# Rotary turns six steps later, a table operation in another step, value evictions on two engines, and the inverse's predicated copies ahead of the low parts

## The chip, the cores and the metric

The kernel runs on one core of a Trainium2 chip. The metric is the time of one execution on the device, in microseconds (us); lower is better. The five engines are named as the profile names them: PE is TensorE (matmuls; PEld are its weight loads), DVE is VectorE, ACT is ScalarE, POOL is GpSimd, and SP is SyncE, which issues the DMAs. Each works through its own queue in order, and they wait for each other on semaphores.

## What is computed

The reference is a two-layer encoder on 256 tokens of width 2048. Each layer normalises, projects all channels by one large matrix, and sends the result to two groups of heads:

```python
for l in range(DEPTH):
    h = rms_norm(x, norm_g[l])
    proj = jnp.einsum('btd,dc->btc', h, w_in[l])
    rw_in, g_rw, q, k_at, v_at, g_at = jnp.split(proj, col_splits, axis=-1)
    ...
    y_rw = rwkv7_branch(r, k, v, xw, xa, ...)
    qh = rope(q.reshape(B, T, AT_HEADS, HEAD_DIM), positions)
    kh = rope(k_at.reshape(B, T, AT_KV_HEADS, HEAD_DIM), positions)
    y_at = window_attention(qh, kh, vh, sink[l]).astype(x.dtype)
    mix = jnp.concatenate([y_rw * jax.nn.silu(g_rw), y_at * jax.nn.silu(g_at)], axis=-1)
    x = x + jnp.einsum('btc,cd->btd', mix, w_out[l])
return rms_norm(x, final_g)
```

The first group is a recurrence over time (16 heads, both directions), the second a windowed attention with rotary positions on q and k: with `t1`, `t2` the halves of a head, the result is `t1 cos - t2 sin` and `t2 cos + t1 sin`.

## The kernel before

**Weights as two parts.** All large products run in a format that keeps fewer bits than float32, so both operands are split in a high and a low part, and each step of a product is three matmuls: high weights by high and by low activations, low weights by high activations (`pm` at L291, L292, L293). A weight tile of 128 rows and 1024 columns arrives by DMA (`raw`, three buffers, L213); `wsplit` then makes its halves: ACT copies 512 columns to `hi` (L221), DVE subtracts to get `lo` (L223). `hi` and `lo` have two buffers each, and one tile feeds eight steps.

**The stream and its windows.** The weight products form one long stream of steps, `S`. The rest (recurrence, attention) is cut into generators. A window runs 64 steps in 14 groups; lists of group numbers say when a generator's next piece is emitted, and TensorE runs in exactly this order (`manual_schedule`). On the other engines a scheduler chooses the order, by the place in the program and by priorities: `tc.high_priority(offset=n)` moves what stands in it ahead, `PRIO_LO = 40` for the low parts and `PRIO_B = 95` for the last stage of the recurrence. What goes through `PA` and `PV` (ACT and DVE by way of `keep_in_program_order`, L236 in the profile) keeps the program's order among itself. `S.later(n, fn)` emits `fn` when n more steps have run.

**The recurrence's inverse.** Ten windows, one for each pair of heads and two for the start, feed three stages: `scan_p` prepares operands, `scan_i` inverts triangular 64x64 blocks, `scan_b` runs the chain over four chunks. The inversion doubles the block size in six levels. Of each level TensorE computes `pq` (L897; transposes at L864), ACT copies it to `QF` (L900) and `tt` (L868), TensorE computes `pd` (L906), and DVE puts `pd` into the block `TC` (tile `tv`) under a mask: `copy_predicated`, L907. The next level's L897 reads `tv`; after the last level L864 does, for `pf`. `scan_b` has `rh` (L956), `suv` (L972 on ACT, L979 on DVE), the product L977, and at its end a variance `yv` (L996, then a power on POOL, L997) and the normalised `ysq`.

**Rotary positions.** When the product of a k or q tile is done, `rope_evac` copies it from PSUM to `raw` (a tile named `u`, L532), issues four DMAs that exchange the halves of the heads into `rrot` (L534, one buffer), and leaves two functions for later: `turn` after 7 steps (two multiplies and an add on DVE) and `parts` after 10 (high part on ACT, low part on DVE). There are ten such tiles in each layer; the next tile's product ends 16 steps after, or 32 where a gate's tile lies between.

**Values.** `v_step` accumulates two tiles `pva` in the two PSUM buffers that all products of the stream share; `v_evac` scales both into `VA` on DVE (L569). The stream's next product takes the first one's buffer.

**Tables.** Sine and cosine are made once, in layer 0, by a generator `setup` of many small DVE operations (tiles `VA`, `SIN`, `COS`); `ROT` and its default list tell in which groups of a window its next operation is emitted.

## Time and profile before

| | us |
|---|---|
| median of three runs | 1202.62 (1201.23 to 1203.34) |
| the profiled execution | 1201.32 |
| its span, first to last instruction | 1199.5 |
| PE busy | 1165.4 |
| DVE busy | 910.2 |
| ACT busy | 776.3 |
| POOL busy | 18.9 |

The granted TensorE clock is 0.991 of full speed on average. A row of the timeline has the start in us, the duration, engine and line, the operation with its output, `<-` and its inputs, the count, and in brackets how long the engine idled before it and what released it. An idle time before a matmul is counted from the modelled end of the one before. `x2` behind a row means two instructions merged, with their joint time.

### The profile page before, as it was taken

How to read it: one execution, taken by the hardware profiler on the slowest of the kernel's cores; microseconds unless marked ns; L12 is line 12 of the kernel's file. 1: busy time of each engine (PE TensorE's matmuls, PEld its weight loads, DVE VectorE, ACT ScalarE, POOL GpSimd, SP SyncE). 2: the span in 40 equal slices, each digit the busy share in tenths (PEclk: the TensorE clock that was granted, in tenths of full speed). 3: DMA queues.
4: the chain of work that ended last, by engine and by line, in shares of the span. 5: the costliest groups of instructions: out<-in, count | busy, mean ns of one | idle time of the engine just before them, and what ended most of it. 6: DMA issues, size and time to landing. Idle time of an engine off the chain costs nothing. (4 is left out here: it accounts for less than half of the span.)

```text
span 1199.5 us, 38085 instructions
## 1 busy us (share of the span) xinstructions
PE 1165.4 (97%) x16151; PEld 1087.2 (91%) x16151; DVE 910.2 (76%) x2019; ACT 776.3 (65%) x1953; POOL 18.9 (2%) x23
## 2 busy tenths in 40 slices
PE   8999999999999999999999999999999999999996
PEld 6998999999888889999999989999998888889996
DVE  6888888888876668866667978887887766786554
ACT  6666776777776557655555766876777665665553
POOL 0000000000000000000000000000000000000000
PEclk8999999999999999999999999999999999999998
DMA  7553333323333434467655443334323333345653
GB/s 254 163 174 124 107 100 114 118 85 115 110 105 106 129 98 137 143 221 249 214 183 166 133 129 113 100 106 127 115 92 99 116 115 131 113 148 186 212 186 121
DMA packets 60410, 166.63 MB, mean 139 GB/s; under 512 B 7728, under 2 KB 22736, under 8 KB 60240
## 3 DMA queue, kind: packets, MB, share of 16 engines
q1 hardware_dynamic: 60240, 164.21, 42.5%
q8 instruction: 126, 2.06, 0.7%
q14 instruction: 44, 0.36, 0.1%
HBM read 157.37 MB, written 4.19 MB: 135 GB/s over the span
## 5 line engine op out<-in xcount | busy, mean ns | idle before, releaser
L291 PE MATMUL pm<-XH,hi 128*128 128x256 f32 x1664 | 495.9, 298 | 3.4 <-ACT XH L183 1.7
L293 PE MATMUL pm<-XH,lo 128*128 128x256 f32 x1664 | 469.9, 282 | 6.2 <-DVE lo L223 6.2
L292 PE MATMUL pm<-XL,hi 128*128 128x256 f32 x1664 | 469.4, 282 | 0.3
L221 ACT ACTIVATE hi<-raw 128x512 fp32r<-128x512 f32 x560 | 327.7, 624 | 194.9 <-PE pm L292 110.3
L223 DVE TENSOR_TENSOR lo<-raw,hi 128x512 fp32r<-128x512 f32 x560 | 369.7, 686 | 97.5 <-ACT hi L221 91.3
L291 PEld LDWEIGHTS pm<-XH,hi 128*128 128x128 f32 x1664 | 315.0, 189 | 18.5 <-ACT XH L183 2.4
L293 PEld LDWEIGHTS pm<-XH,lo 128*128 128x128 f32 x1664 | 315.4, 190 | 8.8 <-DVE lo L223 8.5
L292 PEld LDWEIGHTS pm<-XL,hi 128*128 128x128 f32 x1664 | 315.4, 190 | 1.1 <-DVE XL L184 1.1
L291 PE MATMUL pm<-MH,hi 128*128 128x256 f32 x512 | 144.1, 281 | 0.0
L293 PE MATMUL pm<-MH,lo 128*128 128x256 f32 x512 | 144.0, 281 | 0.0
L292 PE MATMUL pm<-ML,hi 128*128 128x256 f32 x512 | 143.8, 281 | 0.0
L291 PEld LDWEIGHTS pm<-MH,hi 128*128 128x128 f32 x512 | 96.6, 189 | 0.8 <-issue 0.8
L293 PEld LDWEIGHTS pm<-MH,lo 128*128 128x128 f32 x512 | 96.6, 189 | 0.2 <-DVE lo L223 0.2
L292 PEld LDWEIGHTS pm<-ML,hi 128*128 128x128 f32 x512 | 96.6, 189 | 0.0
L907 DVE CAST_PREDICATED tv<-LV,pd 128x256 f16<-128x256 uint8 x80 | 34.4, 430 | 12.8 <-PE pd L906 12.2
L790 DVE TENSOR_TENSOR ge<-pg,C 128x1024 f32<-128x1024 f32 x32 | 38.9, 1221 | 4.4 <-PE pg L784 4.4
L972 ACT ACTIVATE suv<-pcc 64x128 f32<-64x128 f32 x128 | 34.2, 267 | 11.4 <-PE pcc L970 7.1
L900 ACT ACTIVATE QF<-pq 128x256 f16<-128x256 f32 x80 | 30.8, 384 | 14.3 <-PE pq L864 13.8
L1062 ACT ACTIVATE mv<-mv,mx 128x257 f32<-128x257 f32 x64 | 31.8, 501 | 11.3 <-DVE mx L1059 11.3
L956 ACT ACTIVATE rh<-pcc 128x128 f32<-128x128 f32 x64 | 17.5, 273 | 33.2 <-PE pcc L954 32.8
L784 PE MATMUL pg<-mv,bk 64*128 64x128 f32 x512 | 37.2, 285 | 0.3 <-DVE ge L790 0.3
L784 PEld LDWEIGHTS pg<-mv,bk 64*128 64x128 f32 x512 | 31.1, 187 | 2.4 <-DVE ge L790 0.4
(247 smaller groups left out, 1860.1 us busy)
## 6 DMA issues: line engine op xcount, KB each, us to landing
raw<-wi SPq DMA_DIRECT2D x207, 512.0 KB, 3.8
raw<-wo SPq DMA_DIRECT2D x64, 512.0 KB, 4.2
raw<-wv SPq DMA_DIRECT2D x8, 512.0 KB, 3.7
rrot<-u SPq DMA_DIRECT2D x80, 32.0 KB, 2.1
vg<-xT SPq DMA_DIRECT2D x16, 128.0 KB, 4.2
xd<-vg SPq DMA_DIRECT2D x16, 128.0 KB, 3.5
vg<-xd SPq DMA_DIRECT2D x16, 128.0 KB, 3.7
g<-dup SPq DMA_DIRECT2D x16, 97.0 KB
```

The source lines that it names most:

```text
L221: A.activation(hi[:, q], raw[:, q], AF.Copy)
L223: V.tensor_tensor(lo[:, q], raw[:, q], hi[:, q].bitcast(F32), op=ALU.subtract)
L291: PE.matmul(pm, wh, rh[:, kk, :], start=(kk == 0), stop=False)
L292: PE.matmul(pm, wh, rl[:, kk, :], start=False, stop=False)
L293: PE.matmul(pm, wl, rh[:, kk, :], start=False, stop=(kk == 15))
L784: PE.matmul(pg[:, h, c * 128 : (c + 1) * 128], BK[half[h], d, c, 1 - h : 3 - h, :].rearrange("p s j -> p (s j)"), MV[half[h], d, c].rearra ...
L790: V.tensor_tensor(GEd(d), pg.rearrange("p h (c x) -> p h c x", c=NC), gm[d].unsqueeze(1).unsqueeze(1).to_broadcast([128, 2, NC, 128]), op= ...
L900: A.activation(t_sub(QF), flat4(pq[:, :, 0:128]), AF.Copy)
L907: V.copy_predicated(t_sub(TC), t_mask, flat4(pd[:, :, 0:128]))
L956: A.activation(RH, pc[:, 0], AF.Copy)
L972: A.activation(here(h), pc[half[h], 1], AF.Copy)
L1062: A.activation(Sc[:, h, q, 0:257], Sc[:, h, q, 0:257], AF.Exp, scale=0.125, bias=mx[:, q : q + 1], accum_out=den[:, q : q + 1])
```

## The change

```diff
+PRIO_TC = 400
...
-                S.later(7, turn)
-                S.later(10, parts)
+                S.later(13, turn)
+                S.later(15, parts)
...
             L.VA = st("VA", [2, 256])
-            for b in range(2):
-                V.tensor_scalar(L.VA[:, b, :], pvs[b], L.norm.rt[:, b : b + 1], None, op0=ALU.mult)
+            with tc.high_priority(offset=PRIO_B):
+                A.activation(L.VA[:, 0, :], pvs[0], AF.Copy, scale=L.norm.rt[:, 0:1])
+                V.tensor_scalar(L.VA[:, 1, :], pvs[1], L.norm.rt[:, 1:2], None, op0=ALU.mult)
...
-                V.copy_predicated(t_sub(TC), t_mask, flat4(pd[:, :, 0:128]))
+                with tc.high_priority(offset=PRIO_TC):
+                    V.copy_predicated(t_sub(TC), t_mask, flat4(pd[:, :, 0:128]))
...
-            window(64, *scans(w), *([(setup_, ROT.get(w, [3, 6, 9, 12]))] if l == 0 else []))
+            window(64, *scans(w), *([(setup_, ROT.get(w, [3, 6, 12, 12]))] if l == 0 else []))
```

`turn` and `parts` come 6 and 5 steps later. Of the two value tiles ACT evicts the first and DVE the second, both at a raised priority. The five predicated copies of levels two to six have a priority above the low parts and above `scan_b`. In the windows that use the default list (the third to the seventh, counted from one), the table operation of group 9 goes to group 12, where another follows it. The lines of the changed kernel are up to three higher than before, so L907 is L910 there, L223 is L224 and L236 is L237. TensorE's and POOL's instructions keep their order; on SyncE two or three weight loads change places with other DMAs. DVE and ACT change order in the windows concerned.

On DVE at the end of the ninth window of layer 0 (354 to 364 us in the trace) the rows before are these; `u` and `rrot` are the first k tile's rotation, `kd` its low part:

```order
L236 SCALAR_TENSOR_TENSOR lw<-lw,PR,kr 128x256
L996 TENSOR_SCALAR yv<-yv 128x4
L236 TENSOR_TENSOR u<-u,TW 128x256
L236 TENSOR_TENSOR rrot<-rrot,XA 128x256
L236 TENSOR_TENSOR u<-u,rrot 128x256
L223 TENSOR_TENSOR lo<-raw,hi 128x512
L236 TENSOR_TENSOR kd<-u,KA 128x256
L236 TENSOR_TENSOR ysq<-py,yv 128x256
L223 TENSOR_TENSOR lo<-raw,hi 128x512
L907 COPY_PREDICATED tv<-LV,pd 128x2x4x32
```

The same place on DVE in the changed kernel:

```order
L237 SCALAR_TENSOR_TENSOR lw<-lw,PR,kr 128x256
L999 TENSOR_SCALAR yv<-yv 128x4
L237 TENSOR_TENSOR ysq<-py,yv 128x256
L224 TENSOR_TENSOR lo<-raw,hi 128x512 x2
L910 COPY_PREDICATED tv<-LV,pd 128x2x4x32
L237 TENSOR_TENSOR th<-lw,th 128x256
L237 TENSOR_TENSOR u<-u,TW 128x256
L237 TENSOR_TENSOR rrot<-rrot,XA 128x256
L237 TENSOR_TENSOR u<-u,rrot 128x256
```

The rotation moved from ahead of `ysq` and the last copy to behind them.

On DVE in the middle of the third window (104 to 109 us), before; `kr` and `u` are an input tile's eviction and `lw` the bonus of the recurrence:

```order
L236 TENSOR_TENSOR mv<-kr,pp 128x8x64
L433 TENSOR_TENSOR u<-pm,rb 128x256
L907 COPY_PREDICATED tv<-LV,pd 128x2x8x16
L236 TENSOR_TENSOR lw<-lw 128x256
L435 SCALAR_TENSOR_TENSOR kr<-u,PR,kr 128x255
L236 SCALAR_TENSOR_TENSOR lw<-lw,PR,kr 128x256
L436 SCALAR_TENSOR_TENSOR kr<-u,PR,kr 128x255
L223 TENSOR_TENSOR lo<-raw,hi 128x512 x2
```

The same place on DVE in the changed kernel:

```order
L237 TENSOR_TENSOR mv<-kr,pp 128x8x64
L910 COPY_PREDICATED tv<-LV,pd 128x2x8x16
L434 TENSOR_TENSOR u<-pm,rb 128x256
L237 TENSOR_TENSOR lw<-lw 128x256
L224 TENSOR_TENSOR lo<-raw,hi 128x512
L436 SCALAR_TENSOR_TENSOR kr<-u,PR,kr 128x255
L237 SCALAR_TENSOR_TENSOR lw<-lw,PR,kr 128x256
L437 SCALAR_TENSOR_TENSOR kr<-u,PR,kr 128x255
L224 TENSOR_TENSOR lo<-raw,hi 128x512
```

The copy moved ahead of `u`, and one low part ahead of three operations.

On DVE at the end of the fourth window (147 to 153 us), before; `VA` is a table operation of `setup`:

```order
L435 SCALAR_TENSOR_TENSOR kr<-u,PR,kr 128x255
L907 COPY_PREDICATED tv<-LV,pd 128x2x8x16
L436 SCALAR_TENSOR_TENSOR kr<-u,PR,kr 128x255
L236 TENSOR_TENSOR lw<-lw 128x256
L236 SCALAR_TENSOR_TENSOR lw<-lw,PR,kr 128x256
L996 TENSOR_SCALAR yv<-yv 128x4
L236 TENSOR_SCALAR VA<-VA 128x256
L236 TENSOR_TENSOR ysq<-py,yv 128x256
L223 TENSOR_TENSOR lo<-raw,hi 128x512 x2
L907 COPY_PREDICATED tv<-LV,pd 128x2x4x32
```

The same place on DVE in the changed kernel:

```order
L910 COPY_PREDICATED tv<-LV,pd 128x2x8x16
L436 SCALAR_TENSOR_TENSOR kr<-u,PR,kr 128x255
L237 TENSOR_TENSOR lw<-lw 128x256
L437 SCALAR_TENSOR_TENSOR kr<-u,PR,kr 128x255
L237 SCALAR_TENSOR_TENSOR lw<-lw,PR,kr 128x256
L999 TENSOR_SCALAR yv<-yv 128x4
L237 SCALAR_TENSOR_TENSOR VA<-VA 128x256
L237 TENSOR_TENSOR ysq<-py,yv 128x256
L237 TENSOR_SCALAR VA<-VA 128x256
L224 TENSOR_TENSOR lo<-raw,hi 128x512 x2
L910 COPY_PREDICATED tv<-LV,pd 128x2x4x32
```

The first copy moved ahead of `kr`, and there are two table operations, one on either side of `ysq`, where one was.

## The prediction

> **What bounds the kernel now.** I read the page first, then the busy times of two stretches, then the chain of waits with TensorE as the waiting engine.

> ```profile
> span 1199.5 us, 38085 instructions
> PE 1165.4 (97%) x16151; PEld 1087.2 (91%) x16151; DVE 910.2 (76%) x2019; ACT 776.3 (65%) x1953; POOL 18.9 (2%) x23
> ```

> TensorE is busy for 1165.4 of 1199.5 us, and the change leaves its instructions and their order alone. So the time can only fall by what TensorE waits, 34 us with both ends of the program. The waits by releaser:

> ```profile
> PE pm L293 <- DVE lo L223: 6.2, 11, 1.2
> PE pq L897 <- DVE tv L907: 3.5, 8, 0.8
> PE pf L864 <- DVE tv L907: 3.1, 5, 1.5
> PE pcc L977 <- ACT suv L972: 2.7, 2, 1.8
> PE pd L906 <- ACT tt L868: 1.9, 2, 1.0
> PE pm L291 <- DVE VA L569: 1.3, 2, 0.7
> DVE u L236 <- DMA rrot<-u: 17.9, 10, 3.2
> 122.00:288.00 166.00, 165.03 (x3006) 151.89 (x3004) 141.17 (x299) 119.72 (x319) 4.11 (x4) 1.00 0.34 108
> 340.00:420.00 80.00, 74.00 (x1327) 67.62 (x1323) 54.35 (x124) 46.40 (x131) 2.16 (x2) 0.98 0.37 116
> ```

> Columns of a wait: us in total, times, longest. Of a stretch: its length, then busy PE, PEld, DVE, ACT, POOL, the granted clock, the DMA share and GB/s. From 122 to 288 us VectorE is busy for 85% and TensorE hardly waits (0.97 us in 166). From 340 to 420 us, where the rotations of k and q lie, VectorE is busy for 68% and TensorE idles for 6 us. That second stretch is short of order, not of VectorE: the row above the windows says that VectorE stood 17.9 us, in ten waits, before a rotation whose DMA had not landed.

> **The rotations.** Two of the places, in order of time:

> ```profile
> 353.50 0.36 ACT L532 ACTIVATE u<-pm 128x256 f32<-128x256 f32 x1
> 358.87 0.43 DVE L236 TENSOR_TENSOR u<-u,TW 128x256 f32<-128x256 f32 x1 [1.25 <-DMA rrot<-u]
> 361.87 0.42 DVE L907 CAST_PREDICATED tv<-LV,pd 128x256 f16<-128x256 uint8 x1
> 362.35 0.30 PE L864 MATMUL pf<-EYE,tv 64*64 64x32 f16 x16 [1.47 <-DVE tv L907]
> 409.80 0.42 DVE L236 TENSOR_TENSOR u<-u,TW 128x256 f32<-128x256 f32 x1 [2.31 <-DMA rrot<-u]
> 411.05 0.42 ACT L236 ACTIVATE kr<-u 128x256 fp32r<-128x256 f32 x1 [2.96 <-DVE u L236]
> 412.41 0.54 ACT L972 ACTIVATE suv<-pcc 64x128 f32<-64x128 f32 x2
> 413.01 0.39 PE L977 MATMUL pcc<-suv,bt 128*64 128x64 f32 x6 [1.78 <-ACT suv L972]
> ```

> From the copy that feeds the DMAs to the first multiply there are 5.4 us (353.50 to 358.87). The stretch from 122 to 288 us is four windows, 41.5 us each, or 0.65 us for each of a window's 64 steps. Seven steps are 4.6 us: the rotation is placed ahead of its data, and VectorE, in order, holds the copy of L907 and the low parts behind it; at 411 us ScalarE's `kr` waits for the rotation and holds `suv`, and TensorE waits 1.78 us for that. Thirteen steps are 8.5 us, 3 us after the landing. In the new order `ysq`, both low parts and the copy stand ahead of the rotation at 358, and `suv` ahead of `kr` at 411. At 362 the copy loses from ahead of it the wait of 1.25 us and four operations (the rotation's three and the low part `kd`) of some 0.35 us from start to start: 2.6 us, for 1.47 needed. Next late there is `ysq`, which waits for POOL; 1.1 us of such a wait are covered. The rows L864 (3.1), L977 (2.7) and L906 (1.9) go entirely, and 1.6 of L897's 3.5 (what is left of it is below): 9.3 us. Half of it would stay if the freed engines met their next order too late; more than 9.3 can't come from here. The DMAs of a rotation are issued where they were, but for one tile in each layer's attention windows, which SyncE issues one weight load later; its turn comes six steps later as well, so nothing waits for it. POOL's queue is unchanged.

> **The clock.** After the wait of 1.78 us the granted clock fell:

> ```profile
> 413.00:418.00 5.00, 4.99 (x47) 4.64 (x49) 3.34 (x9) 2.15 (x5) 0.00 (x0) 0.66 0.34 105
> ```

> A third of 5 us of matmuls was lost: 1.7 us. With the wait gone, I take the 1.7 us as gained. [...]

> **The values.** Two evictions in a row stand on VectorE, behind a reciprocal:

> ```profile
> 341.63 1.76 DVE L236 RECIPROCAL kd<-pk 128x256 f32<-128x256 f32 x1
> 343.31 0.38 DVE L569 TENSOR_SCALAR VA<-pva,rt 128x256 f32<-128x256 f32 x1
> 343.75 0.39 PE L291 MATMUL pm<-XH,hi 128*128 128x256 f32 x1 [0.66 <-DVE VA L569]
> 342.89 0.28 ACT L956 ACTIVATE rh<-pcc 128x128 f32<-128x128 f32 x1 [1.18 <-PE pcc L954]
> ```

> The next tile takes the first value tile's bank. ScalarE now evicts that one, in the 1.18 us in which it idles before `rh`; a PSUM tile of this size costs it 0.36 us (row at 353.50). It ends about when TensorE arrives: 1.2 of the 1.3 us go. The trace shows no such eviction with a column as scale; if it ran behind `rh` instead, the gain would be half, and a loss has no room, since `rh` moves by at most 0.3 us.

> **The copies' priority in the third window**, where VectorE has no idle time at all:

> ```profile
> 97.00 0.43 DVE L907 CAST_PREDICATED tv<-LV,pd 128x256 f16<-128x256 uint8 x1
> 97.49 0.30 PE L897 MATMUL pq<-tv,AB 64*64 64x32 f16 x16 [0.59 <-DVE tv L907]
> 102.79 0.68 DVE L223 TENSOR_TENSOR lo<-raw,hi 128x512 fp32r<-128x512 f32 x1
> 103.53 0.38 PE L293 MATMUL pm<-XH,lo 128*128 128x256 f32 x1
> 107.59 1.28 DVE L223 TENSOR_TENSOR lo<-raw,hi 128x512 fp32r<-128x512 f32 x2
> 108.32 0.39 PE L293 MATMUL pm<-XH,lo 128*128 128x256 f32 x1 [0.55 <-DVE lo L223]
> ```

> The copy moves ahead of three short operations, so the wait at 97.49 goes. But the low part at 102.79 has the same work before it as ever, and L293 starts 0.74 us after it, the same distance as at 108.32 where it did wait: TensorE arrives earlier and waits there. I count 0 for 97.49, and 0 for its twin in the second layer (685.64, a wait of 0.39 us):

> ```profile
> 685.64 0.23 PE L897 MATMUL pq<-tv,AB 64*64 64x32 f16 x6 [0.39 <-DVE tv L907]
> 696.28 0.38 PE L293 MATMUL pm<-XH,lo 128*128 128x256 f32 x1 [0.52 <-DVE lo L223]
> ```

> At 108.32 the order itself improves: one low part now stands ahead of `kr`, `lw`, `kr`, three operations of the width of the `u` rows above, 0.42 us each. That gives 0.55, and 0.52 at 696.28: 1.1 us. Bounds: 0, and 2.1 with the two that I count at nothing.

> **The table operation and the copies, windows 4 to 7.**

> ```profile
> 147.66 0.42 DVE L907 CAST_PREDICATED tv<-LV,pd 128x256 f16<-128x256 uint8 x1
> 148.13 0.30 PE L897 MATMUL pq<-tv,AB 64*64 64x32 f16 x16 [0.23 <-DVE tv L907]
> 149.32 0.29 DVE L236 TENSOR_SCALAR VA<-VA 128x256 f32<-128x256 f32 x1
> 150.53 0.42 DVE L236 TENSOR_TENSOR ysq<-py,yv 128x256 f32<-128x256 f32 x1 [0.93 <-POOL yv L997]
> 150.88 1.28 DVE L223 TENSOR_TENSOR lo<-raw,hi 128x512 fp32r<-128x512 f32 x2
> 152.08 0.42 DVE L907 CAST_PREDICATED tv<-LV,pd 128x256 f16<-128x256 uint8 x1
> 152.69 0.30 PE L864 MATMUL pf<-EYE,tv 64*64 64x32 f16 x16
> ```

> The copy at 147.66 comes about 0.4 us earlier, and the wait of 0.23 us goes. Asked by stretches of 40 us, the chain of waits has it once in each of the four from 120 to 280, 0.9 us in all:

> ```profile
> PE pq L897 <- DVE tv L907: 0.2, 1, 0.2
> ```

> But the table operation that left its old place now stands between `ysq` and the low parts, behind POOL's result: the one that was there hides in the 0.93 us of idleness, the second does not. The last copy of the window comes 0.2 to 0.34 us later than 152.08, and L864, which follows a copy by 0.47 us at the least (147.66 to 148.13), has only 0.13 us to spare. It then waits, and ends up 0.06 to 0.33 us later than before: over four windows I take a loss of 0.8 us in place of a gain of 0.9. The bounds are these two.

> **The sum.** 9.3 + 1.2 + 1.1 + 1.7 - 0.8 = 12.5 us, less 0.5 for low parts that the new order puts behind the softmax in the attention windows (between 0 and 1.3, one low part of 0.64 us late in each layer): 12.0 us. The profiled execution took 1201.32 us (1.8 around its span) and stands 1.3 us below the median of three, 1202.62. 1201.3 - 12.0 = 1189.3 us. A difference under 0.2% (2.4 us) can't be told from none.

> **Rivals.**
> - *Given back* (0.16). The third window shows how: TensorE arrives early and finds the next operand late, since VectorE's work is the same. If that holds in the rotations' windows too, only half of the 12.0 us stays: 1195.3. Against it: the compressed 340 to 420 us would load VectorE to 54.35 of some 73 us, 74%, where 85% ran without waits.
> - *The clock falls for another reason* (0.11): then 1.7 us stay, 1191.0. [...]
> - *The rotations' buffer* (0.04), the one that ends slower. `rrot` has one buffer and the next rotated tile follows after 16 steps. With the turn at 13, three steps (1.9 us) remain; if VectorE runs it later than that, SyncE stands before the next tile's DMAs, and the weight loads behind them in its queue come late. Ten times in two layers at 1.8 us, the longest wait that TensorE shows, is 18 us against the 12.0 gained: 1207. It decides from a turn that is more than 1.9 us late; that VectorE stands idle for a third of these windows speaks against it.
> - *No difference* (0.05), within 1200.2 to 1205.0: the scheduler's order would have to meet other durations than it assumed, so that the copies stand at the head before their matmuls have run.

> **How the numbers follow.** The forecast has 0.64. Its own range: 1186.0 with every term at its better end (9.3 + 1.3 + 2.1 + 1.7 + 0.9 = 15.3 us); 1192.0 with the clock term and 1 us more of the waits lost. With the two rivals that are faster the range reaches 1196.5. Faster: 0.64 + 0.16 + 0.11 = 0.91; same 0.05; slower 0.04.

> **What would show it.** Right: the wait of VectorE for `rrot` nearly gone; L977 and L906 missing from TensorE's waits; no stretch at half clock around 410 us; a new wait of L864 in the four windows after 122 us; L293's waits in the attention windows still there. Wrong: L293 or L897 waiting more than before between 340 and 520 us; SyncE standing long before `rrot`; ScalarE's `VA` behind `rh`.

## The result and the profile after

The changed kernel takes 1188.21 us (median of 4 runs, 1186.08 to 1189.24) beside 1201.95 us for the kernel before (4 runs, 1201.23 to 1203.34): a ratio of 0.9882, 95% interval 0.9865 to 0.9899, or 13.7 us. In later runs it was 1188.47 us beside 1198.51 (ratio 0.9905, 0.9888 to 0.9922). The changed kernel's two medians agree; those of the kernel before lay between 1198.5 and 1202.0 in four groups of runs, and in one group its runs spread over up to 5.8 us. Part of that spread turns out to belong to the explanation.

The profiled execution of the changed kernel spans 1186.6 us, 12.9 less than before. Its page begins:

```profile
span 1186.6 us, 38095 instructions
...
PE 1160.9 (98%) x16151; PEld 1082.7 (91%) x16151; DVE 908.2 (77%) x2017; ACT 777.3 (66%) x1955; POOL 18.7 (2%) x23
```

The busy times are nearly the old ones; it is TensorE's idleness that shrank. The chain of waits, with TensorE waiting (us in total, times, longest), and VectorE's row for the rotations:

```profile
PE pm L294 <- DVE lo L224: 5.8, 11, 1.2
PE pf L866 <- DVE tv L910: 1.6, 5, 0.4
...
PE pm L292 <- ACT hi L222: 1.4, 2, 0.7
...
PE pm L292 <- DVE VA L571: 0.7, 1, 0.7
...
PE pn L931 <- ACT tt L870: 0.4, 2, 0.2
...
DVE u L237 <- DMA rrot<-u: 4.2, 4, 2.0
```

Lines have moved by one to three: L977 is now L980, L906 is L908, L897 is L899, L864 is L866, L907 is L910. L980, L908 and L899 are gone from the list, VectorE's 17.9 us before the rotations are 4.2, and L866 waits in another place. One wait for `VA` of two is left. The wait of L931 for `tt` (0.4) is new, and L292 waits longer for `hi` (1.4, against 0.4 before).

The stretches, as before (length; busy PE, PEld, DVE, ACT, POOL; granted clock; DMA share; GB/s):

```profile
122.00:288.00 166.00, 164.59 (x3002) 151.20 (x3001) 140.03 (x300) 119.89 (x320) 4.21 (x4) 1.00 0.34 108
339.00:413.00 74.00, 73.07 (x1348) 66.84 (x1343) 54.17 (x124) 47.16 (x133) 2.01 (x2) 1.00 0.41 124
406.00:411.00 5.00, 5.00 (x61) 4.46 (x60) 4.89 (x13) 2.70 (x7) 0.00 (x0) 1.00 0.53 184
```

The rotations' stretch now runs with 0.93 us of idleness in 74, where 6 in 80 were lost, at full clock. VectorE is busy there for 73%, as the prediction had worked out (74%). The two places that it showed, from the timeline in order of time:

```profile
357.85 0.42 DVE L237 TENSOR_TENSOR ysq<-py,yv 128x256 f32<-128x256 f32 x1 [1.18 <-POOL yv L1000]
358.19 1.28 DVE L224 TENSOR_TENSOR lo<-raw,hi 128x512 fp32r<-128x512 f32 x2
359.39 0.42 DVE L910 CAST_PREDICATED tv<-LV,pd 128x256 f16<-128x256 uint8 x1
...
359.86 0.30 PE L866 MATMUL pf<-EYE,tv 64*64 64x32 f16 x16
...
360.06 0.42 DVE L237 TENSOR_TENSOR u<-u,TW 128x256 f32<-128x256 f32 x1
...
405.59 0.54 ACT L975 ACTIVATE suv<-pcc 64x128 f32<-64x128 f32 x2
...
406.84 0.45 PE L980 MATMUL pcc<-suv,bt 128*64 128x64 f32 x8
...
406.91 0.42 ACT L237 ACTIVATE kr<-u 128x256 fp32r<-128x256 f32 x1 [0.34 <-DVE u L237]
```

`ysq`, the low parts and the copy stand ahead of the rotation, which starts without a wait; L866 follows the copy by 0.47 us, the distance at which it starts where it waits, so it doesn't wait, but has nothing to spare. `ysq` waits for POOL, as expected. At the second place `suv` stands ahead of `kr`.

TensorE runs the same instructions in nearly the same order in all kernels here, so two traces can be laid over each other. The table gives the time between the starts of the same TensorE instructions, those that start at 80, 120, 300 us and so on in the first profile of before; "rest" is everything else, the program's ends included.

| us | 80–120 | 120–300 | 335–350 | 350–425 | 665–700 | 905–935 | 935–1003 | rest | span |
|---|---|---|---|---|---|---|---|---|---|
| before | 40.06 | 179.94 | 14.98 | 74.96 | 34.96 | 29.91 | 68.03 | 756.7 | 1199.5 |
| before_2 | 40.09 | 179.82 | 14.95 | 75.28 | 34.94 | 29.91 | 69.07 | 757.1 | 1201.1 |
| before_3 | 40.09 | 179.83 | 14.95 | 73.50 | 34.96 | 29.91 | 68.84 | 756.4 | 1198.5 |
| changed | 39.12 | 179.89 | 14.95 | 68.26 | 34.18 | 29.20 | 64.34 | 756.7 | 1186.6 |
| after_2 | 39.13 | 179.99 | 14.96 | 68.21 | 34.19 | 29.19 | 64.36 | 756.7 | 1186.7 |
| later_only | 40.09 | 179.97 | 14.94 | 68.21 | 34.93 | 29.92 | 64.39 | 756.4 | 1188.8 |
| early | 39.09 | 179.98 | 14.95 | 72.35 | 34.21 | 29.17 | 67.31 | 754.1 | 1191.2 |
| no_prio | 39.88 | 180.67 | 14.99 | 68.17 | 34.93 | 29.18 | 64.37 | 755.4 | 1187.5 |
| va_vec | 39.12 | 179.94 | 14.95 | 68.28 | 34.22 | 29.94 | 64.35 | 755.2 | 1186.0 |
| table_9 | 39.11 | 178.73 | 14.99 | 68.17 | 34.21 | 29.19 | 64.35 | 756.3 | 1185.0 |
| turn_10 | 39.09 | 179.95 | 14.99 | 72.09 | 34.16 | 29.20 | 66.25 | 755.8 | 1191.5 |
| turn_15 | 39.12 | 179.94 | 14.99 | 67.83 | 34.18 | 29.19 | 63.98 | 754.8 | 1184.1 |
| best1 | 39.12 | 178.75 | 14.25 | 68.20 | 34.21 | 29.19 | 64.36 | 755.5 | 1183.6 |
| best2 | 39.14 | 178.87 | 14.25 | 67.85 | 34.19 | 29.19 | 64.00 | 755.3 | 1182.8 |

Where two kernels share the code of a stretch, its length agrees within some 0.1 us, but for the rotations' two stretches in before (73.5 to 75.3 and 68.0 to 69.1). So a difference of 0.3 us in one column is a reading, while "rest" varies by 3 us, most of it in the first 25 us, at 60 to 80 and at 640 to 665 us. In the first 25 us the traces differ in the granted clock: in before, before_2, after_2, later_only and va_vec two stretches of 3.4 us run at half clock (0.50 from 7.55 to 14.37 us in before), in the others one or none. Between before and after: the rotations' columns give 6.7 + 3.7, the two third windows 0.9 + 0.8, the values in the second layer 0.7, windows 4 to 7 nothing, and the values in the first layer nothing.

### The profile page after: what moved, and what is told of

Read it like the earlier page. It is cut to its first block, busy times and chain, and to the rows that moved or that the text cites. A ratio compares the mean times of both kernels' runs of the same rounds, so it can differ in the third digit from the quotient of the medians.

```text
span 1186.6 us, 38095 instructions
## 1 busy us (share of the span) xinstructions
PE 1160.9 (98%) x16151; PEld 1082.7 (91%) x16151; DVE 908.2 (77%) x2017; ACT 777.3 (66%) x1955; POOL 18.7 (2%) x23
## 4 chain that ended last, share of the span: by engine, by line
PE 74%; issue 15%; DVE 7%; ACT 2%; POOL 1%; DMA 1%; SPq 0%; DVEq 0%; POOLq 0%; ACTq 0%
PE pm L292 19%; PE pm L294 16%; PE pm L293 16%; PE pg L786 3%; DVE lo L224 2%; PE pcc L957 2%; PE py L987 2%; PE py L964 1%; PE pcc L980 1%; PE pq L899 1%; PE pcc L970 1%; PE pd L908 1%; PE pza L671 1%; POOL yv L1000 1%; PE pscr L1050 1%
## 5 line engine op out<-in xcount | busy, mean ns | idle before, releaser
L292 PE MATMUL pm<-XH,hi 128*128 128x256 f32 x1664 | 494.2, 297 | 3.9 <-ACT XH L184 1.6
L294 PE MATMUL pm<-XH,lo 128*128 128x256 f32 x1664 | 467.8, 281 | 5.9 <-DVE lo L224 5.8
L293 PE MATMUL pm<-XL,hi 128*128 128x256 f32 x1664 | 467.6, 281 | 0.8 <-DVE XL L185 0.6
L224 DVE TENSOR_TENSOR lo<-raw,hi 128x512 fp32r<-128x512 f32 x560 | 369.1, 686 | 102.5 <-ACT hi L222 95.2
L292 PEld LDWEIGHTS pm<-XH,hi 128*128 128x128 f32 x1664 | 313.4, 188 | 19.3 <-ACT XH L184 2.6
L294 PEld LDWEIGHTS pm<-XH,lo 128*128 128x128 f32 x1664 | 313.9, 189 | 8.3 <-DVE lo L224 8.3
L293 PEld LDWEIGHTS pm<-XL,hi 128*128 128x128 f32 x1664 | 314.1, 189 | 1.7 <-DVE XL L185 1.7
L292 PE MATMUL pm<-MH,hi 128*128 128x256 f32 x512 | 144.0, 281 | 0.0
L294 PE MATMUL pm<-MH,lo 128*128 128x256 f32 x512 | 143.8, 281 | 0.0
L293 PE MATMUL pm<-ML,hi 128*128 128x256 f32 x512 | 143.8, 281 | 0.0
L292 PEld LDWEIGHTS pm<-MH,hi 128*128 128x128 f32 x512 | 96.6, 189 | 0.8 <-issue 0.8
L293 PEld LDWEIGHTS pm<-ML,hi 128*128 128x128 f32 x512 | 96.6, 189 | 0.0
L294 PEld LDWEIGHTS pm<-MH,lo 128*128 128x128 f32 x512 | 96.6, 189 | 0.0
L910 DVE CAST_PREDICATED tv<-LV,pd 128x256 f16<-128x256 uint8 x80 | 34.2, 428 | 12.0 <-PE pd L908 11.4
L902 ACT ACTIVATE QF<-pq 128x256 f16<-128x256 f32 x80 | 30.8, 384 | 12.5 <-PE pq L866 11.7
```

The costliest lines, as they stand in the source:

```text
L224: V.tensor_tensor(lo[:, q], raw[:, q], hi[:, q].bitcast(F32), op=ALU.subtract)
L292: PE.matmul(pm, wh, rh[:, kk, :], start=(kk == 0), stop=False)
L293: PE.matmul(pm, wh, rl[:, kk, :], start=False, stop=False)
L294: PE.matmul(pm, wl, rh[:, kk, :], start=False, stop=(kk == 15))
L902: A.activation(t_sub(QF), flat4(pq[:, :, 0:128]), AF.Copy)
L910: V.copy_predicated(t_sub(TC), t_mask, flat4(pd[:, :, 0:128]))
```

## The experiments

The theory for all: each part is worth what its own waits are worth, since the order of instructions decides, and the rotations make most of it. Each kernel's runs stand beside runs of before on the same chip, whose median is given with them: 1201.05, 1199.37 or 1198.51 us.

**The rotations alone.** The kernel before with

```diff
-                S.later(7, turn)
-                S.later(10, parts)
+                S.later(13, turn)
+                S.later(15, parts)
```

> The kernel before, with the rotations at steps 13 and 15 and nothing else. Theory (order): PE's waits L864, L977, L906 and most of L897's two long ones (0.81, 0.78 us) in the rotation windows go, 9.1 us as the changed kernel's trace has it, and the half clock after 413 us goes with the wait of 1.78 us, 1.5 to 1.7 us: 1201.95 - 10.7 = 1191.3 us, no stretch of half clock between 400 and 425 us. Rival 1 (the clock falls for another reason): 1192.9, half clock still there. Rival 2 (VectorE's work is conserved, half is given back unless the copies also have their priority): 1196 us. The waits L897 at 97, 148, 189, 231, 272 us and L293 at 108 us must be as before, since nothing moved there.

Measured: 1190.40 us (1188.73 to 1191.04), ratio 0.9907 (0.9891 to 0.9922) to the 1201.05 of before. Both rotation columns have the lengths of the changed kernel, 68.21 and 64.39 us, and all other columns those of before. The clock shows nothing under 1.00 there:

```profile
350.00:418.00 68.00, 67.80 (x1196) 62.02 (x1197) 47.26 (x116) 43.30 (x126) 2.01 (x2) 1.00 0.39 125
```

The edit of two numbers gives 10.7 us here, where the whole change gave 13.7 and 10.0. That half of it would be given back is refuted: 0.2 us of idleness are left in 68.

**The rotations back, the rest kept.** The changed kernel with

```diff
-                S.later(13, turn)
-                S.later(15, parts)
+                S.later(7, turn)
+                S.later(10, parts)
```

> The changed kernel with the rotations back at steps 7 and 10; the table, the copies' priority and the values stay changed. Theory (the parts add up): L866, L980, L908 and L899 wait again in the rotation windows, 9.1 us, and the granted clock falls again to half for 3.4 us behind the wait of 1.78 us, 1.5 to 1.7 us more: 1188.2 + 10.7 = 1198.9 us. Rival 1 (the priority takes the copies past the rotation, so that part of the gain is the priority's): under 1196 us. Rival 2 for the clock (the half clock hangs on where a wait falls against a fixed period, not on the wait's length): the wait of 1.78 us is there, and no half clock follows; 1197.3 us.

Measured: 1193.57 us (1192.44 to 1195.15) beside 1199.37 for before, ratio 0.9958 (0.9944 to 0.9972). My theory of parts that add up fell; rival 1 has it. The rotation columns are 72.35 and 67.31 us: 4.1 and 3.0 longer than with the late rotations, where 6.7 and 3.7 were expected of the pair of profiles. Some 1.5 of the 6.7 are the fall of the clock in the first profile of before, which didn't come in `early`; beside before_3, which had no fall either (73.50 and 68.84), the first column is 1.2 us shorter and the second 1.5. VectorE's rows of the timeline, and TensorE's last:

```profile
357.46 0.43 DVE L237 TENSOR_TENSOR u<-u,TW 128x256 f32<-128x256 f32 x1 [1.87 <-DMA rrot<-u]
...
358.60 0.68 DVE L224 TENSOR_TENSOR lo<-raw,hi 128x512 fp32r<-128x512 f32 x1
...
359.54 0.42 DVE L910 CAST_PREDICATED tv<-LV,pd 128x256 f16<-128x256 uint8 x1
359.87 0.42 DVE L237 TENSOR_TENSOR ysq<-py,yv 128x256 f32<-128x256 f32 x1
...
360.00 0.30 PE L866 MATMUL pf<-EYE,tv 64*64 64x32 f16 x16 [1.15 <-DVE tv L910]
```

VectorE still stands before the rotation, but the priority has put the copy ahead of `ysq` and of one low part behind it, and TensorE waits 1.15 us, where the three profiles of before have 1.47, 1.79 and 1.42. The two parts overlap: late rotations alone bring all that is to be had in these stretches, and with them the priority brings nothing more there (68.21 without it, 68.26 with it).

**Somewhat later.** The changed kernel with

```diff
-                S.later(13, turn)
-                S.later(15, parts)
+                S.later(10, turn)
+                S.later(12, parts)
```

> The changed kernel with the rotations at steps 10 and 12. Ten steps are 6.5 us by 0.65 us a step, and the data lands 5.4 us after the copy. Theory (the scheduler's place decides, not the landing alone: in the order of instructions the first rotation still stands ahead of ysq and the copy of L910): of the waits that went, L866's at 360 us comes back with 1.2 to 1.5 us, and in layer two with 1.0, the others stay away: 1188.2 + 2.3 = 1190.5 us. Rival (6.5 is more than 5.4, so all of them stay away): 1188.2 us.

Measured: 1195.16 us (10 runs, 1192.77 to 1197.31), ratio 0.9969 (0.9958 to 0.9981) to the same before. By the medians this is 1.6 us slower than `early`, by the two columns of the profiles 1.3 us faster (72.09 + 66.25 against 72.35 + 67.31), so the two can't be ranked; it is far from the late rotations (68.26 + 64.34). Half of the six steps bring little. The theory had the first layer's wait right and the rest wrong. VectorE's and TensorE's rows of the timeline:

```profile
359.27 0.43 DVE L237 TENSOR_TENSOR u<-u,TW 128x256 f32<-128x256 f32 x1 [2.03 <-DMA rrot<-u]
...
361.82 0.30 PE L866 MATMUL pf<-EYE,tv 64*64 64x32 f16 x16 [1.31 <-DVE tv L910]
...
367.57 0.42 DVE L237 TENSOR_TENSOR u<-u,TW 128x256 f32<-128x256 f32 x1 [2.00 <-DMA rrot<-u]
...
369.58 1.22 DVE L792 TENSOR_TENSOR ge<-pg,C 128x1024 f32<-128x1024 f32 x1
...
370.85 0.46 PE L809 MATMUL pt<-C,vg 64*64 64x64 f32 x16 [0.91 <-DVE ge L792]
```

The rotation is still queued ahead of its data, with 2.0 us of wait. Ten steps are not "6.5 us after the copy" on VectorE: the copy starts at 353.15 us, and VectorE stands ready for the rotation 4.1 us later. Somewhere between 10 and 13 steps the scheduler's order flips. The next rotation now stands ahead of `ge`, and TensorE has a new wait of 0.9 us in each layer.

**Later still.** The changed kernel with

```diff
-                S.later(13, turn)
-                S.later(15, parts)
+                S.later(15, turn)
+                S.later(17, parts)
```

> The changed kernel with the rotations at steps 15 and 17; the next rotated tile takes the one rrot buffer after 16 steps, so one step, 0.65 us, is left for VectorE. Theory (VectorE runs a rotation well within that, and the weight loads behind the transfer in SyncE's queue have slack): 1188.2 us, within 1 us; SyncE's wait ahead of the rrot transfers grows by under 1 us at each. Rival (the one buffer): SyncE stands before the transfers for the rotation's multiply and adds a wait of TensorE for the high parts of the next weight tiles: slower by 0.5 to 1.8 us at each of some ten places, 1193 to 1206 us.

Measured: 1185.73 us (1185.60 to 1187.49), ratio 0.9899 (0.9884 to 0.9914). The rotation columns are 0.4 us shorter each: L931's two waits for `tt`, which ScalarE's `kr` held ahead of it while it waited for a rotation at 13 (0.49 us at 400 us), are gone. What SyncE waited for, in this kernel:

```profile
SPq L535 <- ACT hi L222: 35.1, 12, 8.0
SPq L535 <- DVE u L237: 15.2, 10, 3.4
```

and in the changed kernel:

```profile
SPq L535 <- ACT hi L222: 52.6, 18, 7.6
SPq L535 <- DVE u L237: 8.7, 8, 1.3
```

So the one buffer holds the transfers longer (1.5 us each time, up to 3.4, where it was 1.1 and up to 1.3; "under 1 us" of growth was too little). But these waits stand in part in place of those for `hi`, and TensorE feels nothing of them: the chain of waits has no more than 0.2 us for `hi`. The rival that ends slower is refuted for turns up to 15; a turn at 16 or more would come after the next tile has the buffer, and no run has one. The median is 2.5 us under the 1188.2 expected: the two columns give 0.8 of it, the remainder isn't explained.

**Without the copies' priority.** The changed kernel with

```diff
-PRIO_TC = 400
+PRIO_TC = 0
```

> The changed kernel with the copies' priority offset 0. Theory (the copy's place decides): L899 waits again at 97 us (0.6), 678 us (0.4) and in the four windows after 120 us (0.23 each, 0.9), L294 waits again at 108 and 688 us (0.55 each, 1.1) and no longer at 103.6 and 684.4 us (0.31 and 0.33): 1188.2 + 0.6 + 0.4 + 0.9 + 1.1 - 0.6 = 1190.6 us. Rival (given back: VectorE has no idle time in that window, TensorE is late by the same sum either way): 1188.2 to 1188.8 us.

Measured: 1190.28 us (1189.32 to 1191.18) beside 1201.05, ratio 0.9908 (0.9893 to 0.9923); 1190.6 was expected. By columns 0.76 us are lost in the first layer's third window, 0.75 in the second's, 0.8 in windows 4 to 7. The row that comes back, with a wait in the third window of each layer and in three of windows 4 to 7:

```profile
PE pq L899 <- DVE tv L910: 1.7, 5, 0.6
```

The wait at 103.6 us goes again, as expected: it is the one that the priority creates. In the changed kernel it was

```profile
103.60 0.38 PE L294 MATMUL pm<-XH,lo 128*128 128x256 f32 x1 [0.31 <-DVE lo L224]
```

VectorE's work is conserved (busy for 908.3 us here and 908.2 with the priority), and yet TensorE gains.

**The table operation back.** The changed kernel with

```diff
-            window(64, *scans(w), *([(setup_, ROT.get(w, [3, 6, 12, 12]))] if l == 0 else []))
+            window(64, *scans(w), *([(setup_, ROT.get(w, [3, 6, 9, 12]))] if l == 0 else []))
```

> The changed kernel, with the table operation back in step 9 of a window (3, 6, 9, 12). Theory (place): the four waits of L866 at 152, 193, 235, 276 us (0.27 to 0.44 us, 1.4 in all) come from the second table operation behind POOL's result; they go, and the copy's priority still keeps L899 from waiting: 1188.2 - 1.4 = 1186.8 us. Rival (VectorE is 85% busy there, so the operation costs the same wherever it stands): L866's waits go, and L899's of 0.23 us come back in four windows, with one or two of the low parts' late: 1187.7 to 1188.3 us.

Measured: 1187.23 us (1186.76 to 1187.87), ratio 0.9884 (0.9867 to 0.9901) to 1201.05. Windows 4 to 7 take 178.73 us, 1.2 less than in either kernel of the case. Step 12 of the changed kernel:

```profile
149.47 0.42 DVE L237 TENSOR_TENSOR ysq<-py,yv 128x256 f32<-128x256 f32 x1 [0.90 <-POOL yv L1000]
149.81 0.28 DVE L237 TENSOR_SCALAR VA<-VA 128x256 f32<-128x256 f32 x1
...
151.21 0.42 DVE L910 CAST_PREDICATED tv<-LV,pd 128x256 f16<-128x256 uint8 x1
...
151.68 0.30 PE L866 MATMUL pf<-EYE,tv 64*64 64x32 f16 x16 [0.29 <-DVE tv L910]
```

and of this one:

```profile
148.54 0.42 DVE L237 TENSOR_TENSOR ysq<-py,yv 128x256 f32<-128x256 f32 x1 [0.93 <-POOL yv L1000]
...
150.09 0.41 DVE L910 CAST_PREDICATED tv<-LV,pd 128x256 f16<-128x256 uint8 x1
...
150.56 0.30 PE L866 MATMUL pf<-EYE,tv 64*64 64x32 f16 x16
```

The 0.3 us operation behind `ysq` was the wait. In step 9 it costs nothing: L899 doesn't wait again. So this part of the change is a loss, by 1.2 us in the trace; the timed medians, from different groups of runs, differ by 1.0.

**The values by VectorE alone.** The changed kernel with `v_evac` as before:

```diff
-            with tc.high_priority(offset=PRIO_B):
-                A.activation(L.VA[:, 0, :], pvs[0], AF.Copy, scale=L.norm.rt[:, 0:1])
-                V.tensor_scalar(L.VA[:, 1, :], pvs[1], L.norm.rt[:, 1:2], None, op0=ALU.mult)
+            for b in range(2):
+                V.tensor_scalar(L.VA[:, b, :], pvs[b], L.norm.rt[:, b : b + 1], None, op0=ALU.mult)
```

> The changed kernel with both value tiles evicted by VectorE, without priority, as before. Theory from the two traces: in the second layer TensorE's wait of 0.66 us comes back, in the first layer it waits as long either way (0.66 us, for the tile that VectorE still evicts behind its reciprocal): 1188.2 + 0.7 = 1188.9 us. Rival (the sum on record): both waits were gone by the split, 1189.4 us, and then the first layer's wait would be longer here than 0.66 us.

Measured: 1189.07 us (1187.78 to 1192.99), ratio 0.9901 (0.9884 to 0.9919) to 1201.05; expected 1188.9. The waits, first this kernel's:

```profile
PE pm L292 <- DVE VA L570: 1.3, 2, 0.7
```

The 0.7 us lie in the second layer alone. In the first, the wait stays whoever evicts the first tile. In this stretch of the changed kernel ScalarE has evicted it long before, and TensorE is released by VectorE:

```profile
341.21 0.47 ACT L570 ACTIVATE VA<-pva,rt 128x256 f32<-128x256 f32 x1 [0.43 <-PE pva L563]
...
342.37 0.39 DVE L571 TENSOR_SCALAR VA<-pva,rt 128x256 f32<-128x256 f32 x1
...
342.81 0.38 PE L292 MATMUL pm<-XH,hi 128*128 128x256 f32 x1 [0.66 <-DVE VA L571]
```

In the changed kernel the next product's first matmul waits on VectorE's semaphore in the first layer (for 0.66 us, at 342.81 us) and on ScalarE's in the second (at 921.14 us, where no idleness shows). This points to the second tile's buffer in the first layer and the first tile's in the second; the trace doesn't name the buffer, so that stays an inference.

**Both values by ScalarE, table in step 9.** The table's edit, and in `v_evac`

```diff
-                A.activation(L.VA[:, 0, :], pvs[0], AF.Copy, scale=L.norm.rt[:, 0:1])
-                V.tensor_scalar(L.VA[:, 1, :], pvs[1], L.norm.rt[:, 1:2], None, op0=ALU.mult)
+                for b in range(2):
+                    A.activation(L.VA[:, b, :], pvs[b], AF.Copy, scale=L.norm.rt[:, b : b + 1])
```

> The changed kernel with the table operation back in step 9, and both value tiles evicted by ScalarE at the same priority. Theory (the wait at 342.8 us in the first layer is that of the tile which VectorE evicts behind its reciprocal): that wait of 0.66 us goes, 0.4 to 0.7 us faster than with the table alone: 1187.2 - 0.6 = 1186.6 us. Rival (ScalarE becomes late): the second eviction, 0.4 us, holds rh, and TensorE waits there for rh in both layers: 1187.2 to 1188.0 us.

Measured: 1185.23 us (1184.38 to 1185.77), ratio 0.9890 (0.9874 to 0.9907) to 1199.37; expected 1186.6. The first layer's column falls from 14.95 to 14.25 us, and no other is longer than with the table alone, so `rh` isn't late for TensorE. The 0.7 us are what this edit gives; why the median came out another 1.4 us under the 1186.6 stays open.

**The changed kernel again, and the best version beside it.** The first is unchanged; the second joins the table in step 9, both values by ScalarE, and the rotations at 15 and 17.

> The changed kernel once more, beside the kernel before on this chip. Theory (the two waits of L292 for the high parts, 0.71 us each at 66 and 647 us in the first profile, hang on when a weight load lands in that execution, not on the change): other values there, 0 to 0.4 us, as in the variants of the changed kernel; every other wait within 0.05 us of the first profile; 12.5 to 14 us faster than before. Rival (they are the change's doing): 0.71 us again at both places.

> The changed kernel with the table operation in step 9, both value tiles evicted by ScalarE, and the rotations at steps 15 and 17. Theory (the three add up: 1.2 us for the table, 0.7 for the values, 0.6 for the two waits of L931 for tt that the rotations at 13 brought): 2.5 us faster than the changed kernel in the same call. Rival (given back at the next late operand): under 1.2 us faster.

Measured side by side, with before at 1198.51 us: 1188.47 us (1187.32 to 1189.52) for the changed kernel and 1184.63 (1183.99 to 1185.16) for the best version, ratio 0.9873 (0.9854 to 0.9893). The waits for `hi` at 66 and 647 us, 0.71 each in the first profile, were 0.00 and 0.48 in the second: they vary from one execution to the next, and so aren't the change's. (The waits at the start, for `XH`, vary too, by 0.3 us, where 0.05 was expected.) The gain of 10.0 us fell short of the 12.5 to 14 expected: the changed kernel is where it was, and it is before that ran faster here, whose two rotation columns alone differ by up to 1.8 and 1.0 us between its three profiles. Whether that is all of it stays open, since the sum of the two columns was 143.0 us in the first profile of before and 144.4 and 142.3 in the later ones. The best version is 3.8 us faster than the changed kernel where 2.5 were expected. Its columns give the 2.5 (1.1 + 0.7 + 0.4 + 0.4); the remaining 1.3 us of the two profiles lie in "rest", mostly ahead of 24 us. There after_2 ran two stretches at half clock (8.19 to 15.02 us) and best2 one (8.01 to 11.42), and best2 gains 1.0 us between 10 and 15 us; so that part belongs to the execution. Why the medians of five runs differ by as much stays open. Its longest row of TensorE's waits:

```profile
PE pm L294 <- DVE lo L224: 5.8, 11, 1.2
```

The rows for `tv`, `suv`, `tt` and `VA` are gone from its list; the low parts are left.

**The clock.** The kernel before, two more executions with a profile.

> The kernel before once more, for the clock. Theory A (on record: the half clock follows the wait of 1.78 us): half clock for 3.4 us behind the wait at 411 to 413 us again. [...] The waits themselves as in the first profile.

> The kernel before a third time, for the clock. Theory A: half clock for 3.4 us behind the wait of 1.78 us again. [...]

Measured: 1202.89 and 1200.27 us. In the first trace of before the granted clock is 0.50 from 413.73 us on for 3.413 us, and in the changed kernel's from 10.68 us on for as long. Four stretches of that length in before_2:

```profile
360.74:364.15 3.41, 1.62 (x66) 1.38 (x66) 3.41 (x8) 2.66 (x6) 0.00 (x0) 1.00 0.18 35
364.16:367.57 3.41, 3.41 (x23) 3.19 (x20) 1.71 (x3) 0.43 (x2) 0.00 (x0) 0.50 0.50 163
411.94:415.35 3.41, 1.78 (x20) 1.57 (x22) 2.89 (x8) 1.92 (x6) 0.00 (x0) 1.00 0.06 24
415.35:418.77 3.42, 3.42 (x51) 3.15 (x45) 2.56 (x6) 2.13 (x5) 0.00 (x0) 1.00 0.46 149
```

the two of the first profile of before,

```profile
410.32:413.73 3.41, 1.63 (x25) 1.35 (x24) 2.89 (x8) 2.31 (x6) 0.00 (x0) 1.00 0.00 1
413.73:417.14 3.41, 3.41 (x17) 3.19 (x19) 1.75 (x6) 1.43 (x3) 0.00 (x0) 0.50 0.50 154
```

two of before_3,

```profile
412.12:415.53 3.41, 2.54 (x31) 2.37 (x31) 2.57 (x7) 1.86 (x6) 0.00 (x0) 1.00 0.18 38
415.53:418.95 3.42, 3.42 (x49) 3.05 (x50) 3.39 (x13) 1.32 (x4) 0.00 (x0) 1.00 0.65 196
```

and two of `early`, with its wait of 1.42 us:

```profile
407.56:410.97 3.41, 1.99 (x28) 1.72 (x27) 2.91 (x8) 2.31 (x6) 0.00 (x0) 1.00 0.11 43
410.97:414.38 3.41, 3.41 (x38) 3.07 (x38) 2.56 (x7) 1.74 (x4) 0.00 (x0) 1.00 0.50 154
```

Theory A doesn't hold as it stands: behind the wait near 413 us, 1.63 and 1.67 us long in these two executions, the clock stayed at 1.00. In before_2 it fell elsewhere, behind a wait of 1.79 us at 362, and in before_3 nowhere between 13 and 1190 us. The falls in the first profile of before, at 7.55, 413.73 and 1188.56 us, lie 119 and 227 times 3.413 us apart. A stretch with TensorE busy for 1.62 or 1.63 us of 3.41 (0.48) was followed by one at half clock; those with 1.78 (0.52), 1.99 and 2.54 us were not. In the changed kernel's trace the clock is 1.00 from 14.10 to 1178.04 us.

What sets the clock stays open. The falls at 413.73 and 364.16 us came behind waits of 1.78 and 1.79 us and none behind those of 1.63, 1.67 and 1.42 us, so the length of the single wait fits these executions as well as the busy time of the stretch. And the busy time alone does not tell near the program's start, where in before_3 a stretch with TensorE busy for 2.53 us (0.74) was followed by one at half clock:

```profile
5.94:9.35 3.41, 2.53 (x13) 1.76 (x12) 2.37 (x5) 2.54 (x6) 0.00 (x0) 1.00 1.00 387
9.35:12.77 3.42, 3.42 (x15) 2.92 (x13) 3.19 (x7) 3.42 (x9) 0.00 (x0) 0.50 1.01 408
```

## Why the prediction was right

The forecast was 1189.3 us, within 1.1 us of the 1188.21 measured, and the mechanism is the one forecast: the order of VectorE and ScalarE, not their load. Term by term, in the pair of profiles:

- **Rotations, 9.3 us: 8.9** by the columns (6.7 and 3.7, less the clock's 1.5). L980, L908 and L899 went, with VectorE's wait for `rrot`. L931's two new waits (0.37 and 0.35 by starts) were not foreseen: at 13 steps `kr` still waits for a rotation ahead of `tt`. They are inside the 8.9. The size belongs to this pair: L864's wait at 948 us was 1.01 us here and 1.60 in before_2 and before_3, where VectorE waited 19.2 and 18.8 us for `rrot` instead of 17.9. And the step count was no ground for it: "Thirteen steps are 8.5 us, 3 us after the landing" would by the same reckoning put ten steps (6.5 us) behind the landing at 5.4, and `turn_10` shows the rotation ahead of it. What held is the order of instructions that the prediction also gave.
- **Clock, 1.7 us: 1.5 in this pair, but not in every execution.** "With the wait gone, I take the 1.7 us as gained" is the step that failed: behind the wait near 413 us the clock fell where it was 1.78 us long, and not where it was 1.63 and 1.67. In one of three executions of before there was no fall (73.50 us in the rotations' column against 74.96 and 75.28), so the change brings this part only against some executions; that the first profile had it is luck. The falls of that profile lie whole multiples of 3.413 us apart, and those of before_2 and before_3 at other places (364.16 and 9.35 us); in the stretch ahead of the one at 413.73 us TensorE was busy for 1.63 us of 3.41. More of their cause the runs don't show.
- **Values, 1.2 us: 0.7.** By the waits, "The next tile takes the first value tile's bank" holds in the second layer only. With both tiles on ScalarE the other 0.7 us come too.
- **Third windows, 1.1 us: 1.7.** The waits for the copy went and the low part behind was late by 0.31 and 0.33 us, as argued; but the trade wasn't even. By starts the first layer gains 0.66 + 0.16 + 0.71 and gives back 0.20 + 0.40. Part of the difference is how waits are read: between starts these waits are 0.07 to 0.16 us longer than the idle time shown in brackets (0.59 shown, 0.66 lost; 0.55 shown, 0.71 lost; 0.66 shown for `VA`, 0.73 lost).
- **Table and copies, −0.8 us: 0.0.** The new wait of L866 was there in all four windows (0.27 to 0.44 us), but the column is unchanged within 0.05 us: the copies' gain of 0.30 us in each window (L899, by starts) stands against it, with small gains behind. Taken back alone, the table operation gives 1.2 us (`table_9`), and the priority costs 0.8 (`no_prio`). I had taken the loss without the gain.
- **Low parts in the attention windows, −0.5 us:** no loss shows.

The terms measured make 8.9 + 1.5 + 0.7 + 1.7 = 12.8 us beside the 12.9 between the two spans and the 12.0 forecast. Three terms came out 0.2 to 0.5 us smaller and three 0.5 to 0.8 larger, so the sum is better than its parts. That "rest" is 756.7 us in both profiles is luck too, since it varies by 3 us; beside before in the later runs the gain was 10.0 us. Of the rivals, "given back" is refuted by `later_only`, the buffer by `turn_15`, and "the clock falls for another reason" is partly true.

What the prediction had no idea of: the rotations and the priority do in part the same work (`early`), and the gain doesn't grow with the steps: ten are hardly better than seven.

## What to carry to other kernels

A delay given in steps is a wish to the scheduler: look up where the operation lands in its engine's queue, ahead of which others, and against when its data lands; between two values the gain can be little or all. An edit of several parts is worth testing part by part even where the sum is right: here one part cost 1.2 us, two overlapped, and one worked in one layer of two, so that the best version is faster than the change, by 2.5 us in the columns and 3.8 in the timed medians. Lay the traces over each other by the instructions of the engine that never changes its order: its stretches repeat to 0.1 us, where whole runs vary by 3 to 6.
